# One core, a two-block network: the experts' gate and up products with 512 columns, and partial sums joined by products with stacked identities

## The chip, the cores and the metric

The kernel runs on one core of one Trainium2 chip. The metric is the device time of one launch in microseconds (us). Engines: TensorE (PE in the profile, PEld its weight loads), VectorE (DVE), ScalarE (ACT), GpSimd (POOL), SyncE (SP, which here issues nearly all transfers from memory).

## What is computed

256 tokens of width 1024 pass through two blocks. The first ends in a mixture of 32 experts, which is what the change touches; the second (retention and pooling, feed-forward, convolution, feed-forward) follows it. Each token goes to 2 of the 32 experts:

```python
xb = xf[toks]
hid = jax.nn.silu(xb @ w_exp_gate[e]) * (xb @ w_exp_up[e])
return hid @ w_exp_down[e]
```

Here `xb` is (tokens, 1024), gate and up are (1024, 512), down is (512, 1024), all in 32-bit floats. The three weights of one expert are 6 MB, those of all experts 201 MB, and every launch reads all of them.

## The kernel before

Every expert gets 32 slots (CAP); a branch after the eighth expert (LAST = 7, lines 1667 to 1670) handles experts with more tokens and is not entered with these inputs. For four experts together `gather` (line 1533) builds a one-hot matrix `oh` and turns 4 x 32 token rows into the stationary operand `xe` with the model width on the partitions: eight slices of 128 rows, 32 columns for each expert. `scales` (line 1555) makes the row scale and the gate weight of every slot.

**Gate and up.** `inward` (line 1571) runs once for gate (columns 0:128 of the bank `gu`) and once for up (128:256), and takes two loads of 1 MB each time (`kh`, half of the 1024 rows). TensorE's array is used as four quarters of 32 columns. Before the change quarter n of the array makes output columns n of four: each of the 8 row slices is loaded as weights into all four quarters and each quarter multiplies 128 weight columns. That is 32 products of 128 columns for gate and 32 for up, for each expert; a product in 32-bit floats is two instructions in the trace. The result has the 32 slots of quarter n on partitions 32n to 32n+31. Silu on ACT (line 1657) and a product on DVE (line 1658) make `hd`; `turn` (line 1580) transposes it with one product and a DVE copy to `ht`, the stationary operand of the down product.

**Down.** `down` (line 1587) takes two loads, 16 products of 256 columns in all. `scaled` (line 1594) splits the result into a rounded part (ACT, line 1599) and the rest (DVE, line 1600), four times each, in turn. Once for four experts `scatter` (line 1608, tile `wt`) and `add` (line 1616) put the rows back to their tokens in the banks `y`.

**Order.** The loop over experts runs gate(e), turn(e-1), up(e), then `finish(e-1)`, that is down(e-1). A scheduler sets the order of instructions on each engine inside the loop by its own estimates; an engine then takes them strictly in that order. From line 1675 on (`manual_schedule`) the order is as written: the tail of expert 31 and the start of the retention stage. Between the loop and the tail `tables` (line 1686) computes the sine tables on DVE and ACT (18 DVE instructions, lines 1692 to 1706).

**Loads.** `expert_loads` (line 1508) gives the order of the 1 MB loads: gate, gate, up, up of expert e, then down, down of expert e-1; the very last load is cut in two. SP issues them (line 295) into a ring of 1 MB places, as soon as the place's former content has been used. PSUM has four banks (`pw`) for all of this besides the four `y` banks, taken in turn; the pool `hid` holds one buffer each of `hd`, `ht` and `wt`.

Of the kernel before, what the change touches and what calls it, by code (L numbers as in the profile page):

```python
# [11 lines left out]
AF = mybir.ActivationFunctionType  # L12
OP = mybir.AluOpType
# [7 lines left out]
LAST = 7  # L21
# [142 lines left out]
class Block:  # L164
# [1362 lines left out]
    def experts(self):  # L1527
# [43 lines left out]
        def inward(xe, pg, at):  # L1571
            for kh in range(2):
                w = self.next_weights().rearrange("p k (h c t) -> p k h t c", h=2, t=2)
                for k in range(4):
                    for n in range(4):
                        nc.tensor.matmul(pg[quarter(n), at:at + 128], lhsT=xe[:, 4 * kh + k],  # L1576
                                         rhs=w[:, k, n // 2, n % 2], start=(at == kh == k == 0),
                                         stop=(at > 0 and kh == 1 and k == 3))

        def turn(hd):  # L1580
            pt = self.bank("hT")
            nc.tensor.transpose(pt[:, 0:128], hd, c("ident"))
            ht = tile(self.hid, "ht", 256)[:, 0:128]
            nc.vector.tensor_copy(ht, pt[:, 0:128])
            return ht

        def down(ht, pd, half, ahead=0):
            wd = self.next_weights(ahead)
            for k in range(2):
                for n in range(4):  # L1590
                    nc.tensor.matmul(pd[n % 2][quarter(n), 0:256], lhsT=ht[:, quarter(2 * half + k)],  # L1591
                                     rhs=wd[:, k, n * 256:(n + 1) * 256], start=(half + k == 0), stop=(half == k == 1))

# [8 lines left out]
        def outward(e, ht, gs, ye):  # L1602
            pd = [self.bank("dn")] * 2
            for half in range(2):
                down(ht, pd, half, len(self.places) - 2 if e == LAST and half else 0)
# [18 lines left out]
        group = None  # L1624

        def finish(e, ht, oh, gs):
# [5 lines left out]
            outward(e, ht, gs, group)  # L1632
# [3 lines left out]
        hd = mine = None  # L1636
        for e in range(32):
            of = mine
# [8 lines left out]
            xs = xe[:, :, quarter(e % 4)]  # L1647
            pg = self.bank("gu")
            inward(xs, pg, 0)
            if e % 4 == 0:  # L1650
                gs, scale = scales(e, oh)
                mine = oh, gs
            ht = None if hd is None else turn(hd)
            inward(xs, pg, 128)
            now = tile(self.hid, "hd", 256)[:, 0:128]
            sc = scale[:, e % 4:e % 4 + 1]
            nc.scalar.activation(now, pg[:, 0:128], AF.Silu, scale=sc)  # L1657
            nc.vector.scalar_tensor_tensor(now, pg[:, 128:256], sc, now, op0=OP.mult, op1=OP.mult)  # L1658
            if e == 31:
                nc.gpsimd.tensor_tensor(self.rows[:, 1], self.rows[:, 0], self.rows[:, 1], op=OP.mult)  # L1660
            if ht is not None:
                finish(e - 1, ht, *of)
            hd = now
# [691 lines left out]
```

## Time and profile before

| | |
|---|---|
| median of 3 runs | 1380.73 us (1380.12 to 1380.96) |
| profiled execution | 1378.72 us |
| its span | 1376.8 us, so 1.9 us lie outside it |
| PE busy | 1230.7 us (89%) |
| PE weight loads | 1023.2 us (74%) |
| DVE busy | 769.3 us (56%) |
| ACT busy | 539.6 us (39%) |
| expert weights read | 201 MB of 355 MB |
| PE products of gate and up (line 1576) | 4096 instructions, 168.9 us busy |

The page divides the span into 40 slices of 34 us. A row of windows gives, for each stretch, the busy time of each engine with the number of instructions in brackets, then the granted clock of TensorE as a share of 2.4 GHz, the busy share of the DMA engines and the rate of transfers. A row of a timeline gives start and length in us, engine, line, operation, tiles, how often, and in square brackets how long the engine had been idle before and what it waited for. The expert stage lies between about 347 and 791 us.

### The profile page before, as it was taken

The numbers are of one execution on the slowest core, as the hardware profiler recorded it, in microseconds if no ns is written. First come the engines' busy times: TensorE is split into PE (matmuls) and PEld (weight loads), VectorE is DVE, ScalarE is ACT, GpSimd is POOL, SyncE is SP. The second block draws the span as 40 slices with busy tenths as digits, with TensorE's granted clock in tenths as the row PEclk, the third lists the DMA queues.
The fourth block names the chain that finished last, engine by engine and source line by source line (L and its number), as shares of the span: only waits on it lengthen the run. The fifth ranks groups of instructions, "written<-read, shape, count | busy, mean of one in ns | idle before, by whom it ended". The sixth has DMA issues, their size and how long they took to land.

```text
span 1376.8 us, 28610 instructions
## 1 busy us (share of the span) xinstructions
PE 1230.7 (89%) x12204; PEld 1023.2 (74%) x12204; DVE 769.3 (56%) x1559; ACT 539.6 (39%) x884; POOL 147.0 (11%) x124
## 2 busy tenths in 40 slices
PE   8999999999886777676767699999999999999997
PEld 7989888898765455444535499788888997888886
DVE  5577547876332132131212386877776789766665
ACT  4553533554221111121111274354555535555553
POOL 1022201002000000000000032012221200111112
PEclk9999989999997877888868799999999999999999
DMA  7535513996999999999999998365556268665520
GB/s 213 184 115 158 159 40 128 356 411 253 385 417 416 418 418 420 418 419 418 419 419 418 381 301 292 102 230 184 184 192 190 78 162 266 207 195 195 191 77 31
DMA packets 146455, 360.10 MB, mean 262 GB/s; under 512 B 6672, under 2 KB 101904, under 8 KB 121744
## 3 DMA queue, kind: packets, MB, share of 16 engines
q1 hardware_dynamic: 144800, 353.69, 69.5%
q0 software_dynamic: 1376, 4.25, 1.0%
q8 instruction: 97, 1.59, 0.5%
q14 instruction: 38, 0.31, 0.1%
q10 hardware_dynamic: 144, 0.26, 0.0%
HBM read 354.92 MB, written 3.26 MB: 260 GB/s over the span
## 4 chain that ended last, share of the span: by engine, by line
PE 41%; DMA 24%; DVE 3%; ACT 1%; issue 0%; SPq 0%; ACTq 0%; DVEq 0%
PE f L445 11%; DMA raw<-in_w_exp_down_dram 10%; DMA raw<-in_w_exp_gate_dram 7%; DMA raw<-in_w_exp_up_dram 6%; PE f L446 6%; PE f L468 3%; PE f L467 3%; PE f L469 3%; PE cv L2105 2%; PE first L452 1%; PE v L469 1%; PE v L467 1%; PE v L468 1%; PE gu L1576 1%; PE xe L1545 1%; PE r L468 1%
## 5 line engine op out<-in xcount | busy, mean ns | idle before, releaser
L323 DVE TENSOR_TENSOR wlo<-raw,whi 128x1024 fp32r<-128x1024 f32 x231 | 292.4, 1273 | 151.8 <-ACT whi L321 146.5
L321 ACT ACTIVATE whi<-raw 128x1024 fp32r<-128x1024 f32 x238 | 249.9, 1057 | 220.5 <-PE f L445 87.7
L445 PE MATMUL f<-hT,whi 128*128 128x512 f32 x672 | 236.3, 395 | 0.0
L1576 PE MATMUL gu<-raw,xe 128*32 128x128 f32 x4096 | 168.9, 312 | 53.5 <-DMA raw<-in_w_exp_up_dram 33.4
L1576 PEld LDWEIGHTS gu<-raw,xe 128*32 128x32 f32 x4096 | 130.9, 122 | 92.2 <-DMA raw<-in_w_exp_up_dram 43.4
L446 PE MATMUL f<-hT,wlo 128*128 128x256 f32 x672 | 188.4, 280 | 0.0
L445 PEld LDWEIGHTS f<-hT,whi 128*128 128x128 f32 x672 | 126.0, 188 | 29.4
L1600 DVE SCALAR_TENSOR_TENSOR ye<-dn,gs,ye 32x256 fp32r<-32x256 f32 x128 | 61.5, 481 | 134.5 <-ACT ye L1599 133.8
L1599 ACT ACTIVATE ye<-dn,gs 32x256 fp32r<-32x256 f32 x128 | 59.6, 465 | 174.8 <-PE dn L1591 118.3
L446 PEld LDWEIGHTS f<-hT,wlo 128*128 128x128 f32 x672 | 127.0, 189 | 0.8
L1591 PE MATMUL dn<-raw,ht 128*32 128x256 f32 x1024 | 85.1, 460 | 45.3 <-DMA raw<-in_w_exp_down_dram 37.7
L1591 PEld LDWEIGHTS dn<-raw,ht 128*32 128x32 f32 x1024 | 34.2, 124 | 82.2 <-DMA raw<-in_w_exp_down_dram 29.6
L1658 DVE SCALAR_TENSOR_TENSOR hd<-gu,scale,hd 128x128 f32<-128x128 f32 x32 | 11.2, 350 | 106.6 <-ACT hd L1657 106.5
L1657 ACT ACTIVATE hd<-gu,scale 128x128 f32<-128x128 f32 x32 | 11.8, 367 | 149.8 <-PE gu L1576 149.8
L1948 POOL TENSOR_TENSOR fs<-fs,r 128x512 f32<-128x512 f32 x22 | 39.3, 1787 | 290.0 <-ACT fs L1947 290.0
L467 PE MATMUL f<-whi,fa 128*128 128x512 f32 x176 | 69.3, 394 | 0.0
L468 PE MATMUL f<-whi,fa 128*128 128x512 f32 x176 | 69.0, 392 | 0.2 <-DVE fa L342 0.2
L469 PE MATMUL f<-wlo,fa 128*128 128x512 f32 x176 | 68.7, 390 | 0.0
L1545 PEld LDWEIGHTS xe<-oh,xn 128*128 128x128 f32 x256 | 36.8, 231 | 12.9 <-issue 12.1
L1545 PE MATMUL xe<-oh,xn 128*128 128x128 f32 x256 | 39.0, 320 | 6.5 <-PEq L1669 5.7
L429 PE MATMUL gt<-hT,whi 128*128 128x256 f32 x128 | 38.7, 303 | 0.0
L467 PEld LDWEIGHTS f<-whi,fa 128*128 128x128 f32 x176 | 33.1, 188 | 7.6 <-ACT fa L341 0.5
(618 smaller groups left out, 2547.3 us busy)
## 6 DMA issues: line engine op xcount, KB each, us to landing
raw<-in_w_exp_gate_dram SPq DMA_DIRECT2D x64, 1024.0 KB, 19.9
raw<-in_w_exp_up_dram SPq DMA_DIRECT2D x64, 1024.0 KB, 19.9
raw<-in_w_exp_down_dram SPq DMA_DIRECT2D x63, 1024.0 KB, 20.0
raw<-in_ffn_w_gate_dram SPq DMA_DIRECT2D x22, 1024.0 KB, 5.4
raw<-in_ffn_w_up_dram SPq DMA_DIRECT2D x22, 1024.0 KB, 5.3
raw<-in_ffn_w_down_dram SPq DMA_DIRECT2D x22, 1024.0 KB, 4.8
raw<-in_w_in_dram SPq DMA_DIRECT2D x20, 1024.0 KB, 5.3
raw<-in_conv_w_pw_dram SPq DMA_DIRECT2D x12, 1024.0 KB, 5.5
```

The lines of the kernel that those rows point to most:

```text
L321: nc.scalar.activation(hi, raw[:, k:k + step], AF.Copy)
L323: self.los.append(eng.tensor_tensor(lo, raw[:, k:k + step], hi.bitcast(F32), op=OP.subtract))
L445: nc.tensor.matmul(ps[cb], lhsT=whi[:, k, s], rhs=self.two[n][:, :, kk], start=f, stop=False)
L446: nc.tensor.matmul(ps[cb][:, 1], lhsT=wlo[:, k, s], rhs=self.two[n][:, 0, kk], start=False, stop=l)
L467: nc.tensor.matmul(ps[tt], lhsT=hi[:, k0 + k, s], rhs=whi[:, k, cols], start=f, stop=False)
L468: nc.tensor.matmul(ps[tt], lhsT=lo[:, k0 + k, s], rhs=whi[:, k, cols], start=False, stop=False)
L469: nc.tensor.matmul(ps[tt], lhsT=hi[:, k0 + k, s], rhs=wlo[:, k, cols], start=False, stop=l)
L1545: nc.tensor.matmul(ps[:, a], lhsT=xn[:, tt, d * 128:(d + 1) * 128], rhs=oh[:, tt].rearrange("p e s -> p (e s)"), start=(tt == 0), stop=(tt ...
L1576: nc.tensor.matmul(pg[quarter(n), at:at + 128], lhsT=xe[:, 4 * kh + k], rhs=w[:, k, n // 2, n % 2], start=(at == kh == k == 0), stop=(at > ...
L1591: nc.tensor.matmul(pd[n % 2][quarter(n), 0:256], lhsT=ht[:, quarter(2 * half + k)], rhs=wd[:, k, n * 256:(n + 1) * 256], start=(half + k = ...
L1599: nc.scalar.activation(hi, part, AF.Copy, scale=gs[q])
L1600: nc.vector.scalar_tensor_tensor(lo, part, gs[q], hi.bitcast(F32), op0=OP.mult, op1=OP.subtract)
```

## The change

Gate and up are computed with the other split. Quarter k of the array now takes row slice k of the four in a load, and multiplies all 512 weight columns; so a load needs 4 products of 512 columns instead of 16 of 128. Each quarter then holds a partial sum over a quarter of the rows, in a bank of its own for gate (`pg`) and for up (`pu`). `joined` copies half a bank (256 columns, every second one, with the row scale) to `hd` in SBUF, on ACT for gate and on DVE for up, and returns two products: 128 columns of the copy as the stationary operand, times the constant `rep4`, four identities of 32 stacked on the partitions. Such a product adds the four quarters and turns the result at once. `hidden` applies silu on ACT and the product with up on DVE, and gives `ht` directly; `turn` is gone. `both` runs all of that for one expert, with the down product of the expert before it between the two halves of up (`outward` and `finish` have become generators for this). The loads, their order and their number are the same.

```diff
@@ -1568,20 +1568,30 @@
                 nc.vector.tensor_copy(gs[quarter(a)], ps[quarter(a), a:a + 1])
             return gs, scale
 
-        def inward(xe, pg, at):
-            for kh in range(2):
-                w = self.next_weights().rearrange("p k (h c t) -> p k h t c", h=2, t=2)
+        def inward(xe, pg, halves=(0, 1)):
+
+            for kh in halves:
+                w = self.next_weights()
                 for k in range(4):
-                    for n in range(4):
-                        nc.tensor.matmul(pg[quarter(n), at:at + 128], lhsT=xe[:, 4 * kh + k],
-                                         rhs=w[:, k, n // 2, n % 2], start=(at == kh == k == 0),
-                                         stop=(at > 0 and kh == 1 and k == 3))
-
-        def turn(hd):
-            pt = self.bank("hT")
-            nc.tensor.transpose(pt[:, 0:128], hd, c("ident"))
+                    nc.tensor.matmul(pg[quarter(k)], lhsT=xe[:, 4 * kh + k], rhs=w[:, k], start=(kh == 0), stop=(kh == 1))
+
+        def joined(e, ps, pg, h, by_act):
+
+
+            p = tile(self.hid, "hd", 256)
+            src, sc = pg[:, h * 256:h * 256 + 256].rearrange("p (c t) -> p t c", t=2), scale[:, e % 4:e % 4 + 1]
+            view = p.rearrange("p (t c) -> p t c", t=2)
+            if by_act:
+                nc.scalar.activation(view, src, AF.Copy, scale=sc)
+            else:
+                nc.vector.tensor_scalar(view, src, sc, None, op0=OP.mult)
+            return lambda: [nc.tensor.matmul(ps[:, quarter(2 * h + t)], lhsT=p[:, t * 128:(t + 1) * 128], rhs=c("rep4"),
+                                             start=True, stop=True) for t in range(2)]
+
+        def hidden(ps):
             ht = tile(self.hid, "ht", 256)[:, 0:128]
-            nc.vector.tensor_copy(ht, pt[:, 0:128])
+            nc.scalar.activation(ht, ps[:, 0:128], AF.Silu)
+            nc.vector.tensor_tensor(ht, ht, ps[:, 128:256], op=OP.mult)
             return ht
 
         def down(ht, pd, half, ahead=0):
@@ -1590,6 +1600,20 @@
                 for n in range(4):
                     nc.tensor.matmul(pd[n % 2][quarter(n), 0:256], lhsT=ht[:, quarter(2 * half + k)],
                                      rhs=wd[:, k, n * 256:(n + 1) * 256], start=(half + k == 0), stop=(half == k == 1))
+
+        def both(e, xs, between=lambda: None, then=lambda: None):
+            pg, pu, ps = self.bank("gu"), self.bank("gu"), self.bank("hT")
+            inward(xs, pg)
+            between()
+            for h in range(2):
+                add = joined(e, ps[:, 0:128], pg, h, True)
+                inward(xs, pu, (h,))
+                add()
+            for h in range(2):
+                add = joined(e, ps[:, 128:256], pu, h, False)
+                then()
+                add()
+            return hidden(ps)
 
         def scaled(e, pd, gs, ye):
             q = quarter(e % 4)
@@ -1601,8 +1625,9 @@
 
         def outward(e, ht, gs, ye):
             pd = [self.bank("dn")] * 2
-            for half in range(2):
-                down(ht, pd, half, len(self.places) - 2 if e == LAST and half else 0)
+            down(ht, pd, 0)
+            yield
+            down(ht, pd, 1, len(self.places) - 2 if e == LAST else 0)
             scaled(e, pd, gs, ye)
 
         def scatter(oh):
@@ -1629,13 +1654,13 @@
                 group = tile(self.ye, "ye", 2048, F32R).rearrange("p (m d) -> p m d", m=2)
             if e % 4 == 3:
                 wt = scatter(oh)
-            outward(e, ht, gs, group)
+            yield from outward(e, ht, gs, group)
             if e % 4 == 3:
                 add(e - 3, wt, group)
 
-        hd = mine = None
+        ht = mine = None
         for e in range(32):
-            of = mine
+            of, steps = mine, iter(())
             if e % 4 == 0:
                 xe, oh = gather(e)
                 if not e:
@@ -1644,27 +1669,25 @@
                 self.rows = self.beside("rows", self.t8).rearrange("p (n d) -> p n d", n=2)
                 for n, ap in enumerate((i["norm_final"], i["mixer_norm_g_2"][0])):
                     nc.gpsimd.dma_start(out=self.rows[:, n], in_=ap.partition_broadcast(128))
-            xs = xe[:, :, quarter(e % 4)]
-            pg = self.bank("gu")
-            inward(xs, pg, 0)
-            if e % 4 == 0:
-                gs, scale = scales(e, oh)
-                mine = oh, gs
-            ht = None if hd is None else turn(hd)
-            inward(xs, pg, 128)
-            now = tile(self.hid, "hd", 256)[:, 0:128]
-            sc = scale[:, e % 4:e % 4 + 1]
-            nc.scalar.activation(now, pg[:, 0:128], AF.Silu, scale=sc)
-            nc.vector.scalar_tensor_tensor(now, pg[:, 128:256], sc, now, op0=OP.mult, op1=OP.mult)
+
+            def between():
+                nonlocal gs, scale, mine
+                if e % 4 == 0:
+                    gs, scale = scales(e, oh)
+                    mine = oh, gs
+
+            gs, scale = (None, None) if e == 0 else (gs, scale)
+            if ht is not None:
+                steps = finish(e - 1, ht, *of)
+            ht = both(e, xe[:, :, quarter(e % 4)], between, lambda: next(steps, None))
+            for _ in steps:
+                pass
             if e == 31:
                 nc.gpsimd.tensor_tensor(self.rows[:, 1], self.rows[:, 0], self.rows[:, 1], op=OP.mult)
-            if ht is not None:
-                finish(e - 1, ht, *of)
-            hd = now
             if e == LAST:
-                finish(e, turn(hd), *mine)
-                hd = None
-            if e == LAST:
+                for _ in finish(e, ht, *mine):
+                    pass
+                ht = None
                 most = nc.values_load(self.most[0:1, 0:1], min_val=0, max_val=T)
                 with self.tc.If(most > CAP):
                     self.overflow()
@@ -1675,7 +1698,7 @@
         self.region = self.tc.manual_schedule(engines={PE, ACT, DVE, POOL})
         self.region.__enter__()
         oh, gs = mine
-        ht, wt = turn(hd), scatter(oh)
+        wt = scatter(oh)
         pd = [self.bank("dn") for _ in range(2)]
         for half in range(2):
             down(ht, pd, half)
```

On PE this is expert 30, with no gather in it (two gate loads, two up loads, the two down loads of expert 29; `gu`, `hT`, `dn` are the PSUM banks, `raw` a load), before:

```order
L1576 MATMUL gu<-raw,xe 32x128 x16
L1582 MATMUL hT<-cst,hd 128x128
L1576 MATMUL gu<-raw,xe 32x128 x48
L1591 MATMUL dn<-raw,ht 32x256 x16
```

and with the change:

```order
L1576 MATMUL gu<-raw,xe 32x512 x12
L1588 MATMUL hT<-cst,hd 128x32 x4
L1576 MATMUL gu<-raw,xe 32x512 x4
L1588 MATMUL hT<-cst,hd 128x32 x4
L1601 MATMUL dn<-raw,ht 32x256 x16
```

The gate and up products have gone from 64 to 16; one transpose has become eight products with `rep4`, in two places with four in a row, and all of them stand ahead of the down products of the expert before.

On PE the end of the stage, from the gate and up products of expert 31 on, before:

```order
L1576 MATMUL gu<-raw,xe 32x128 x16
L1582 MATMUL hT<-cst,hd 128x128
L1576 MATMUL gu<-raw,xe 32x128 x48
L1591 MATMUL dn<-raw,ht 32x256 x8
L1582 MATMUL hT<-cst,hd 128x128
L1611 MATMUL wt<-cst,oh 128x128 x2
L1591 MATMUL dn<-raw,ht 32x256 x24
L1620 MATMUL y_3917<-ye,wt 128x512
```

and with the change:

```order
L1576 MATMUL gu<-raw,xe 32x512 x12
L1588 MATMUL hT<-cst,hd 128x32 x4
L1576 MATMUL gu<-raw,xe 32x512 x4
L1588 MATMUL hT<-cst,hd 128x32 x4
L1601 MATMUL dn<-raw,ht 32x256 x8
L1636 MATMUL wt<-cst,oh 128x128 x2
L1601 MATMUL dn<-raw,ht 32x256 x24
L1645 MATMUL y_3917<-ye,wt 128x512
```

The transpose of expert 31 that stood between the two halves of down(30) is gone, and eight products with `rep4` stand ahead of both halves, four of them behind all of up.

On DVE the same end of the stage, from the last instructions of the sine tables (`raw`) on, before:

```order
L1700 SCALAR_TENSOR_TENSOR raw<-raw 128x256
L1701 SCALAR_TENSOR_TENSOR raw<-raw 128x256
L1704 TENSOR_SCALAR raw<-raw 128x256
L1706 TENSOR_SCALAR raw<-raw,cst 128x256
L1658 SCALAR_TENSOR_TENSOR hd<-gu,scale,hd 128x128
L1584 COPY ht<-hT 128x128
L1600 SCALAR_TENSOR_TENSOR ye<-dn,gs,ye 32x256 x8
L1718 TENSOR_TENSOR xg<-y_3917,rows 128x512
```

and with the change:

```order
L1723 SCALAR_TENSOR_TENSOR raw<-raw 128x256
L1724 SCALAR_TENSOR_TENSOR raw<-raw 128x256
L1727 TENSOR_SCALAR raw<-raw 128x256
L1729 TENSOR_SCALAR raw<-raw,cst 128x256
L1587 TENSOR_SCALAR hd<-gu,scale 128x256 x2
L1624 SCALAR_TENSOR_TENSOR ye<-dn,gs,ye 32x256
L1594 TENSOR_TENSOR ht<-ht,hT 128x128
L1624 SCALAR_TENSOR_TENSOR ye<-dn,gs,ye 32x256 x7
L1741 TENSOR_TENSOR xg<-y_3917,rows 128x512
```

Behind the tables stood the product that makes `hd` of expert 31; now the two copies of up's halves stand there, and the product that makes `ht` comes behind the first `ye` instruction of expert 30.

## Rows read from the trace of the kernel before

**Rows 1.** The page, part 2: 40 slices of the span, busy tenths.

```profile
DMA  7535513996999999999999998365556268665520
```

**Rows 2.** Windows: busy of PE, PEld, DVE, ACT, POOL; granted clock; DMA share; GB/s.

```profile
700.00:750.00 50.00, 36.71 (x581) 25.50 (x585) 11.41 (x39) 7.66 (x17) 0.00 (x0) 0.80 1.01 418
...
780.00:785.00 5.00, 4.35 (x51) 2.28 (x43) 3.15 (x10) 1.20 (x3) 0.00 (x0) 0.50 0.90 344
785.00:790.00 5.00, 3.68 (x45) 1.41 (x48) 1.73 (x4) 1.90 (x5) 0.00 (x0) 0.86 0.87 304
```

**Rows 3.** Chain of waits that ended last: start, length, what; 454 to 791 us.

```profile
454.73 19.84 DMA raw<-in_w_exp_down_dram
...
772.22 17.54 DMA raw<-in_w_exp_down_dram
789.80 0.71 PE dn L1591 x8
```

**Rows 4.** Waits of SP, 340 to 360 us: us in total, times, longest.

```profile
SPq L295 <- PE gu L1576: 16.1, 6, 12.0
```

**Rows 5.** Windows of 1 us at the first expert, columns as in rows 2.

```profile
351.00:352.00 1.00, 1.00 (x34) 0.96 (x37) 0.35 (x2) 0.41 (x1) 0.00 (x0) 1.00 0.12 49
352.00:353.00 1.00, 1.00 (x40) 0.84 (x32) 0.00 (x0) 0.00 (x0) 0.00 (x0) 1.00 0.02 8
```

**Rows 6.** Timeline of PE at the first two experts, 350 to 364 us.

```profile
350.61 0.31 PE L1454 MATMUL count<-row,cst 128*128 128x32 f32 x2
350.75 0.39 PE L1455 MATMUL count<-row,cst 128*128 128x32 f32 x2
351.07 2.05 PE L1576 MATMUL gu<-raw,xe 128*32 128x128 f32 x64
353.05 0.61 PE L1559 MATMUL gs<-chosen,oh 128*128 128x4 f32 x4
...
357.88 0.33 PE L1582 MATMUL hT<-cst,hd 128*128 128x128 f32 x1
358.14 2.05 PE L1576 MATMUL gu<-raw,xe 128*32 128x128 f32 x64
360.01 1.91 PE L1591 MATMUL dn<-raw,ht 128*32 128x256 f32 x32
361.73 2.44 PE L1576 MATMUL gu<-raw,xe 128*32 128x128 f32 x64
```

**Rows 7.** Timeline of all engines at the stage's end, experts 30 and 31.

```profile
774.75 1.77 PE L1576 MATMUL gu<-raw,xe 128*32 128x128 f32 x32 [0.16 <-DMA raw<-in_w_exp_gate_dram]
...
776.59 0.29 DVE L1692 CAST raw<-pos 128x256 f32<-128x256 int32 x1 [0.95 <-PE gu L1576]
...
779.74 1.93 PE L1576 MATMUL gu<-raw,xe 128*32 128x128 f32 x32 [1.38 <-DMA raw<-in_w_exp_up_dram]
...
783.17 0.36 DVE L1706 TENSOR_SCALAR raw<-raw,cst 128x256 f32<-128x256 f32 x1 [0.48 <-ACT raw L1705]
...
783.56 0.35 DVE L1658 SCALAR_TENSOR_TENSOR hd<-gu,scale,hd 128x128 f32<-128x128 f32 x1
...
784.19 0.48 PE L1582 MATMUL hT<-cst,hd 128*128 128x128 f32 x1
...
784.46 0.63 PE L1611 MATMUL wt<-cst,oh 128*128 128x128 f32 x2
...
785.02 1.75 PE L1591 MATMUL dn<-raw,ht 128*32 128x256 f32 x16
...
789.80 0.64 PE L1591 MATMUL dn<-raw,ht 128*32 128x256 f32 x8 [0.68 <-DMA raw<-in_w_exp_down_dram]
...
790.37 2.65 DVE L1600 SCALAR_TENSOR_TENSOR ye<-dn,gs,ye 32x256 fp32r<-32x256 f32 x5 [0.53 <-ACT ye L1599]
```

**Rows 8.** Groups by line, 400 to 860 us: busy, mean ns of one, idle before.

```profile
L1584 DVE COPY ht<-hT 128x128 f32<-128x128 f32 x27 | 7.9, 292 | 23.7 <-PE hT L1582 19.7 <-PE dn L1591 3.6
...
L1550 DVE COPY xe<-xe 128x512 f32<-128x512 f32 x6 | 4.1, 692 | 32.7 <-PE xe L1545 32.7
```

## The prediction, made before the changed kernel ran

> **What bounds the kernel now.** I read the page's slices first, then windows, then the chain of waits, then SP's waits and the timeline at both ends of the expert stage. The slices show the DMA engines full in fourteen slices in a row, where the experts are [rows 1]. Windows inside say it in numbers: from 700 to 750 us the DMA share is 1.01 at 418 GB/s, while PE is busy 36.7 of 50 us at a granted clock of 0.80 (it goes between full, 2.4 GHz, and half, 1.2), DVE 11.4 and ACT 7.7 [rows 2]. The chain agrees: from 454.73 us on it runs through expert loads, and leaves them only at 789.80 us, for the last eight instructions of the last down product [rows 3]. So the stage lasts as long as its bytes: six loads of 1 MB (1.05 million bytes each) for one expert, 6.29 MB at 418 GB/s, 15.05 us; 2.5 us for one load. What PE does in between counts only in two places: at the start, where the transfers wait for the first free places, and at the end, behind the last loads.
>
> At the start SP waits 16.1 us for the gate and up products of line 1576, once 12.0 us [rows 4]: the ring is full until the first expert has used its first load. The DMA engines then stand nearly still, at shares of 0.12 and 0.02 in the microseconds from 351 to 353 [rows 5]. That gap of 2 us is all the stream has to gain.
>
> **The products.** Prices at full clock come from the first two experts [rows 6]. Now 64 instructions of 128 columns take 1.98 us (351.07 to 353.05), 31 ns each, so a load (32) 0.99 and an expert (128) 3.96. The down products, 256 columns on the same four quarters, take 1.72 us for 32 (360.01 to 361.73), 53.8 ns each. With 512 columns I take twice that, 107.5 ns: eight instructions for a load, 0.86 us, 3.44 for an expert. That is 0.52 less. The transpose took 0.26 (357.88 to 358.14) and goes. The four joins come: each is two products with 128x128 weights and 32 columns, four instructions. The nearest row has that very form, the four instructions of the two `count` lines with the way back to the quarters, 0.46 us (350.61 to 351.07). Four joins are 1.84. So PE has 0.52 + 0.26 = 0.78 less and 1.84 more, 1.06 us more for each expert, at full clock.
>
> At one place a rule speaks against the change. The row shows 0.26 us for a single transpose between two runs of quarter products, while one of the `count` instructions takes 0.46 / 4 = 0.115, so at most 0.15 us goes into changing from quarters to the whole array and back; the change does this four times in an expert instead of once [rows 6]. The Trainium skill (TensorEngine Tiling (Array Packing), Tiling Modes) says that a change of the tiling mode drains the engine. The trace agrees with a small price; by it two joins at the end would be up to 0.3 us dearer, which the range below holds anyway.
>
> **In the stage.** These 1.06 us lie beside the loads: a plain expert took PE 3.96 + 0.26 + 1.72 = 5.9 us and takes 7.0, of 15.05. At half clock it is 14.0, and the joins add waits, since `hd` has one buffer and PE must wait there for ACT or DVE to copy. A copy of 128x256 from PSUM lies between 0.29 us (128x128) and 0.69 (128x512), by columns 0.43 [rows 8]. Four of these with handovers are some 2.4 us, so at half clock PE would need about 16.4 and fall behind a little; it then stands idle less, and in these rows the clock comes back after full stretches (0.50, then 0.86) [rows 2]. I cost the stage at nothing: the cover is the 15.05 us of loads. Without it the price would be 32 x 1.06 = 34 us. ACT's and DVE's added copies are free in the same way.
>
> **At the start** the first place comes free after eight instructions instead of 32, 0.86 us for 0.99: the stream starts 0.13 us earlier, and everything behind it. Bounds are 0 and -0.13, since no place can be free before the first product has run. I take -0.1. Places two to four come free within 0.5 us of where they did, and 2.5 us of transfer for each covers that.
>
> **At the end** there is no cover. Before, DVE works through the sine tables from 776.59 us, when the second gate load of expert 31 is used up (774.75 + 1.77 = 776.52), to 783.53 [rows 7]. The up products were done at 781.67, yet `hd` starts at 783.56: it stands behind the tables on DVE. What follows is short, because the first half of down(30) does not need it; the second half ends at 785.02 + 1.75 = 786.77, and from there the `ye` instructions, ACT and DVE in turn, set the end: the last one of DVE ends at 793.02, 6.25 us later [rows 7]. The last load arrives at 789.80 and only just does not matter.
>
> With the change the two copies of up stand at the place of `hd` behind the tables, each with its join, and **both halves of down(30) stand behind the second join on PE**. So I count from the end of the tables to the end of down(30). The tables start when the second gate load is used up: at half clock 0.86 x 2 = 1.72 us after 774.75, as now, end 783.5; at full clock 0.86 after, end 782.6. I take 783.0. Then come two copies, 0.86; two joins, 0.92 at full clock, 1.84 at half if everything doubles, between them 1.4 (the transposes `wt` cost 0.56 for two at half clock, 784.46 to 785.02, hardly more than the single one at full); the first half of down(30), 0.86 or 1.75; `wt`, 0.28 or 0.56; the second half, 0.86 or 1.75; and four handovers. One is 0.28 us (DVE's `hd` ends at 783.91, PE starts at 784.19), one 0.03 (783.53 to 783.56); I take 0.15 each, 0.6.
>
> - All at full clock: 782.6 + 0.86 + 0.92 + 0.86 + 0.28 + 0.86 + 0.6 = 787.0, 0.2 us later than 786.77.
> - All at half clock: 783.5 + 0.86 + 1.84 + 1.75 + 0.56 + 1.75 + 0.6 = 790.9, 4.1 later.
> - Half clock up to the first half of down(30), full behind it: 783.0 + 0.86 + 1.4 + 1.75 + 0.28 + 0.86 + 0.6 = 788.75, 2.0 later.
>
> I take the third: the clock is 0.50 from 780 to 785 now and 0.86 in the next 5 us [rows 2], and PE has more waits there than before. Silu and the product for `ht` fit into the gaps between the `ye` instructions of ACT and DVE, and down(31) is ready before its `ye` turn comes, so the 6.25 us stay. Behind them nothing is changed, and the next stage starts from these rows, so the delay goes through. Sum: -0.1 + 2.0 = +1.9 us. Made against the profiled 1378.72 us (span 1376.8) it gives 1380.6; the median of the runs stands 2.0 above that execution, and I add the difference to the median: 1380.73 + 1.9 = **1382.6**.
>
> **Rivals.**
> - *The added products keep the clock up.* Then the end costs 0.2 us and the start gives back 0.1: 1380.8, no change. For it: the clock rises after busy stretches in these rows, and PE has 1.06 us more to do for an expert. Against it: from 776 to 783 PE would wait for loads and copies. The Trainium skill (TensorE: Matmul & The Clock Gate, Why this matters for your kernels) advises to keep TensorE continuously busy and free of gaps; by it the added products would hold the clock up to the end, and the time would be this rival's; no run here shows that yet.
> - *Slower, by the tail at half clock.* Both joins and both down halves at half clock, 4.1 us; if down(31) runs at half clock too, its 1.72 us for a half come twice behind `ht`, and the `ye` of expert 31 wait another 1.3. That gives 1384.7 to 1386.0. It decides from a delay of 2.8 us on, which is 0.2%, about what a measurement of this kernel can tell from no change. For it: 0.50 now at just that place.
> - *The four quarters do not run side by side with 512 columns.* Then one instruction takes 0.43 us (107.5 x 4) and an expert 32 x 0.43 = 13.8 instead of 3.4: PE needs 17.4 us or more against 15.05, and the stage grows by 32 x 2.3 = 75 us. Against it: the down products do run side by side at 256 columns.
> - *Faster.* The tail gets shorter only if down(30) no longer stands behind the tables, and the start gap of 2 us only closes with an earlier first product. Neither is in the change.
>
> **How the numbers follow.** Forecast 0.52 (1380.9 to 1384.1), clock stays up 0.20, tail at half clock 0.22, quarters in a row 0.02, faster for a reason I do not see 0.04. Of the forecast's share about 0.09 lies above +2.8 us. Slower: 0.22 + 0.02 + 0.09 = 0.33; faster 0.04; same 0.63. The range leaves out the quarters in a row and the far ends of both sides: 1379.5 to 1386.0.
>
> **What would show it.** In the changed kernel's trace: eight instructions of 512 columns in about 0.86 us at full clock; a DMA share near 1.0 from 354 us to the last load and that load within 0.3 us of 789.8; the first copy of up for expert 31 right behind the sine tables on DVE; the end of down(30) at 788 to 790; and the whole delay of the last `ye` found again at the span's end. It is wrong if the last load itself moves by over 1 us, if SP waits for products in the middle of the stage, or if down(30) ends before 786.8.

## The result, and the profile after

The changed kernel took 1396.43 us, the median of four runs (1387.28 to 1400.24), beside 1380.42 us for the kernel before: a ratio of 1.0113 [1.0089, 1.0137], 16 us slower. The forecast was 1382.6 with a range up to 1386.0, so the time lies outside, on the slow side, and no rival gave it either. The profiled execution, the slowest of the four, took 1400.24 us; its span is 1398.4 us, 21.6 more than the 1376.8 of before.

The page of the changed kernel, part 2 (40 slices of the span; the clock granted to TensorE and the DMA share) and part 4 (shares of the chain that ended last):

```profile
PEclk9999989999996997676788799999999999999999
DMA  6545515987999999999999767365556358655620
...
PE 39%; DVE 4%; ACT 2%; DMA 1%; issue 1%; DVEq 0%; ACTq 0%; SPq 0%
```

The DMA engines are full through the experts' slices, as in [rows 1], but transfers no longer carry the chain: 1% of the span, where [rows 3] run from load to load for 335 us. Windows of the changed kernel, columns as in [rows 2]:

```profile
700.00:750.00 50.00, 41.74 (x312) 22.09 (x312) 13.03 (x34) 12.03 (x28) 3.47 (x3) 0.83 1.01 418
...
785.00:790.00 5.00, 5.00 (x40) 2.71 (x44) 0.00 (x0) 0.30 (x1) 0.00 (x0) 0.50 1.03 323
...
795.00:800.00 5.00, 1.63 (x12) 0.68 (x12) 4.43 (x14) 0.54 (x2) 0.00 (x0) 0.82 0.05 17
800.00:805.00 5.00, 3.18 (x20) 2.46 (x24) 1.32 (x3) 0.29 (x1) 0.00 (x0) 0.50 0.00 0
```

From 700 to 750 us the stream is as full as before (1.01, 418 GB/s). By 795 to 800 us it is empty (0.05). In the trace the last expert load is issued at 767.70 us and lands 17.6 us later, at 785.3, 4.5 us *earlier* than before (789.75); PE then still has all the products of expert 31 and the down products of experts 29 and 30 ahead of it. So the loads were in time and PE was late. PE's waits between 351 and 790 us show when that came about (us in all, times, longest). Before:

```profile
PE dn L1591 <- DMA raw<-in_w_exp_down_dram: 37.7, 34, 2.8
PE gu L1576 <- DMA raw<-in_w_exp_up_dram: 33.4, 30, 2.7
PE gu L1576 <- DMA raw<-in_w_exp_gate_dram: 17.3, 22, 1.4
```

and the changed kernel:

```profile
PE hT L1588 <- DVE hd L1587: 25.3, 41, 0.7
PE hT L1588 <- ACT hd L1585: 22.0, 30, 1.6
```

PE waited 88.4 us for loads before, and now not once for long enough to be listed; it waits 47.3 us for the copies into `hd`. **PE's spare time, 88.4 us or 2.8 for an expert, was used up.** Groups by line over 16 experts show by what (from expert 12 to expert 28; busy us, mean ns, idle before). Before, 486.5 to 729.9 us:

```profile
L1576 PE MATMUL gu<-raw,xe 128*32 128x128 f32 x2020 | 90.4, 329 | 36.1 <-DMA raw<-in_w_exp_up_dram 23.5 <-DMA raw<-in_w_exp_gate_dram 12.3
L1591 PE MATMUL dn<-raw,ht 128*32 128x256 f32 x512 | 44.7, 476 | 26.3 <-DMA raw<-in_w_exp_down_dram 25.0 <-DVE ht L1584 1.2
L1545 PE MATMUL xe<-oh,xn 128*128 128x128 f32 x128 | 20.3, 323 | 0.0
L1620 PE MATMUL y<-ye,wt 128*128 128x512 f32 x32 | 11.8, 472 | 4.8 <-ACT ye L1599 4.8
L1582 PE MATMUL hT<-cst,hd 128*128 128x128 f32 x16 | 5.6, 349 | 0.0
```

and the changed kernel, 499 to 747.6 us:

```profile
L1576 PE MATMUL gu<-raw,xe 128*32 128x512 f32 x508 | 73.1, 678 | 0.0
L1601 PE MATMUL dn<-raw,ht 128*32 128x256 f32 x512 | 50.8, 555 | 0.0
L1588 PE MATMUL hT<-cst,hd 128*128 128x32 f32 x256 | 48.9, 320 | 34.2 <-DVE hd L1587 17.9 <-ACT hd L1585 15.8 <-DVE ye L1624 0.5
```

The products fell from 90.4 to 73.1 us, the transposes' 5.6 went, the joins cost 48.9 busy and 34.2 of waiting, and the unchanged down products rose from 44.7 to 50.8 at a lower clock (0.77 for 0.80). In all PE was busy 173.0 us of 243.4 before and 205.3 of 248.6 after: 2.0 us more for an expert, and 2.1 more of waits ahead of joins. The two together, 4.1, are more than these same experts waited for loads before: 60.8 us (23.5 + 12.3 + 25.0), 3.8 for an expert, beside the stage's mean of 2.8. The 0.3 beyond is what the pace shows: 248.6 / 16 = 15.5 us for an expert, before 243.4 / 16 = 15.2.

These 16 experts are not the whole loss. Compare the start of the first gate-weight product (`gs`) of an expert in the two traces: that of expert 8 comes 20.8 us later than before (462.94 for 442.11), that of expert 12 12.6, of expert 16 8.0, of expert 28 17.7. PE falls behind already ahead of the branch, makes up a part behind it, and loses it again.

### The profile page after: what moved, and what is told of

It reads as the page before. It is cut to its first block, busy times and chain, and to the rows that moved or that the text cites. A ratio compares the mean times of both kernels' runs of the same rounds, so it can differ in the third digit from the quotient of the medians.

```text
span 1398.4 us, 23663 instructions
## 1 busy us (share of the span) xinstructions
PE 1292.4 (92%) x9612; PEld 1001.4 (72%) x9612; DVE 787.8 (56%) x1591; ACT 566.5 (41%) x948; POOL 147.2 (11%) x124
## 5 line engine op out<-in xcount | busy, mean ns | idle before, releaser
L1588 PEld LDWEIGHTS hT<-cst,hd 128*128 128x128 f32 x512 | 78.5, 219 | 129.3 <-DVE hd L1587 66.9
L1576 PE MATMUL gu<-raw,xe 128*32 128x512 f32 x1024 | 144.3, 655 | 0.0
L1588 PE MATMUL hT<-cst,hd 128*128 128x32 f32 x512 | 92.5, 308 | 54.4 <-DVE hd L1587 30.5
L1601 PE MATMUL dn<-raw,ht 128*32 128x256 f32 x1024 | 94.7, 517 | 2.9 <-issue 2.9
L1587 DVE TENSOR_SCALAR hd<-gu,scale 128x256 f32<-128x256 f32 x64 | 30.9, 484 | 116.3 <-PE gu L1576 65.9
L1576 PEld LDWEIGHTS gu<-raw,xe 128*32 128x32 f32 x1024 | 29.3, 118 | 48.4 <-issue 36.5
L1585 ACT ACTIVATE hd<-gu,scale 128x256 f32<-128x256 f32 x64 | 30.4, 474 | 68.3 <-PE gu L1576 28.1
L1545 PEld LDWEIGHTS xe<-oh,xn 128*128 128x128 f32 x256 | 38.5, 240 | 11.8 <-issue 10.9
```

The source lines that it names most:

```text
L1545: nc.tensor.matmul(ps[:, a], lhsT=xn[:, tt, d * 128:(d + 1) * 128], rhs=oh[:, tt].rearrange("p e s -> p (e s)"), start=(tt == 0), stop=(tt ...
L1576: nc.tensor.matmul(pg[quarter(k)], lhsT=xe[:, 4 * kh + k], rhs=w[:, k], start=(kh == 0), stop=(kh == 1))
L1588: return lambda: [nc.tensor.matmul(ps[:, quarter(2 * h + t)], lhsT=p[:, t * 128:(t + 1) * 128], rhs=c("rep4"), start=True, stop=True) for ...
```

## Where one expert loses the time

The changed kernel on PE and on the engines that make `hd`, one plain expert in the scheduler's order (timeline, columns as in [rows 7]):

```profile
643.61 0.47 ACT L1585 ACTIVATE hd<-gu,scale 128x256 f32<-128x256 f32 x1 [0.91 <-PE hT L1588]
644.14 0.63 PE L1588 MATMUL hT<-cst,hd 128*128 128x32 f32 x4 [0.62 <-ACT hd L1585]
644.70 1.06 PE L1576 MATMUL gu<-raw,xe 128*32 128x512 f32 x8
645.89 0.48 DVE L1587 TENSOR_SCALAR hd<-gu,scale 128x256 f32<-128x256 f32 x1 [8.38 <-PE gu L1576]
646.43 0.63 PE L1588 MATMUL hT<-cst,hd 128*128 128x32 f32 x4 [0.67 <-DVE hd L1587]
647.10 0.48 DVE L1587 TENSOR_SCALAR hd<-gu,scale 128x256 f32<-128x256 f32 x1 [0.72 <-PE hT L1588]
647.64 0.71 PE L1588 MATMUL hT<-cst,hd 128*128 128x32 f32 x4 [0.58 <-DVE hd L1587]
648.28 3.48 PE L1601 MATMUL dn<-raw,ht 128*32 128x256 f32 x32
```

The two joins of up stand one behind the other. The first needs a copy that cannot start before up's last product, the second one that cannot start before the first join has read the single `hd`; so PE stands still 0.67 and 0.58 us, with both halves of the down product, ready to run, queued behind. The granted clock changes in the next stretches. Windows of 1 us behind it, the changed kernel:

```profile
649.00:650.00 1.00, 1.00 (x14) 0.40 (x10) 0.00 (x0) 0.00 (x0) 0.00 (x0) 0.50 1.03 426
650.00:651.00 1.00, 1.00 (x16) 0.54 (x12) 0.00 (x0) 0.00 (x0) 0.00 (x0) 0.50 1.00 418
...
652.00:653.00 1.00, 1.00 (x16) 0.36 (x12) 0.66 (x2) 0.62 (x3) 0.00 (x0) 1.00 1.02 426
...
655.00:656.00 1.00, 0.11 (x1) 0.11 (x2) 0.48 (x1) 0.81 (x2) 0.00 (x0) 1.00 1.02 426
...
659.00:660.00 1.00, 0.35 (x5) 0.23 (x2) 0.48 (x1) 0.00 (x0) 0.00 (x0) 0.50 1.05 434
```

The gaps fall into microseconds at full clock, and the dense down product behind them (649 to 651) gets half. The clock comes back behind it (652) just as the next wait comes (655), and is gone at 659. So it was 0.77 over these 16 experts, 0.80 before, although PE was busy 83% of the time and not 71% (206.7 and 178.4 us of the 250 from 500 to 750).

## The experiments

Four theories. WAITS: the waits for `hd`, set by the order, use up PE's time. PRICE: the joins themselves do. CLOCK: half clock doubles what PE has to do, and without it there would be room. TAIL: the sine tables ahead of the last joins. Each run stands beside runs of the kernel before in its own session. "Pace" is the time from the first gate-weight product (`gs`) of expert 0 to that of expert 28, divided by 28, in the profiled execution.

| run | median us | ratio to before | span | pace | clock 500 to 750 |
|---|---|---|---|---|---|
| before | 1380.42 | | 1376.8 | 13.46 | 0.81 |
| the change | 1396.43 | 1.0113 [1.0089, 1.0137] | 1398.4 | 14.13 | 0.77 |
| written order | 1374.19 | 0.9979 [0.9962, 0.9996] | 1373.4 | 13.52 | 0.80 |
| written order, again | 1377.41 | 0.9994 [0.9984, 1.0004] | 1375.7 | 13.46 | 0.79 |
| joins back to back | 1405.72 | 1.0178 [1.0155, 1.0201] | 1405.9 | 14.34 | 0.83 |
| no branch | 1415.25 | 1.0275 [1.0233, 1.0318] | 1411.3 | 14.66 | 0.76 |
| two buffers, no branch | 1380.72 | 1.0004 [0.9991, 1.0016] | 1377.2 | 13.30 | 0.81 |
| half joins | 1379.00 | 0.9989 [0.9979, 0.9998] | 1375.7 | 13.45 | 0.81 |
| three dummies a join | 1387.21 | 1.0045 [1.0022, 1.0068] | 1386.4 | 13.66 | 1.00 |
| written order, four dummies | 1386.12 | 1.0042 [1.0027, 1.0058] | 1384.6 | 13.89 | 0.99 |
| no tables | 1395.42 | 1.0113 [1.0059, 1.0167] | 1397.1 | 14.14 | 0.77 |
| written order, no tables | 1376.77 | 0.9991 [0.9980, 1.0003] | 1373.7 | 13.46 | 0.84 |

**PE's order as written.** Nothing else is changed; one half of down(e-1) then stands ahead of each join of up.

```diff
-            ht = both(e, xe[:, :, quarter(e % 4)], between, lambda: next(steps, None))
-            for _ in steps:
-                pass
+            with self.tc.manual_schedule(engines={PE}):
+                ht = both(e, xe[:, :, quarter(e % 4)], between, lambda: next(steps, None))
+                for _ in steps:
+                    pass
```

> The changed kernel with PE's order in the expert loop as it is written (gate, half of up, join, half of up, join, half of down, join, half of down, join) instead of the scheduler's order, which puts two joins back to back from expert 13 on. Theory WAITS: PE became the bound of the stage because in back-to-back joins it waits 0.6 us each time for the copy into the one buffer hd, and at half clock besides; it needs 16.2 us for an expert there against 15.05 us of loads. In the written order the copies lie beside other products, a plain expert takes 8 us (as experts 9 to 11 do in the changed kernel), PE catches up and waits for loads again: 1381 to 1387 us. Rival PRICE: the joins' own instructions are too dear in any order: no change, 1390 to 1400 us.

The loss is gone with the same instructions and the same prices; 1374.19 us is even below the expected interval. One expert of this kernel, PE's timeline at half clock:

```profile
635.23 1.06 PE L1588 MATMUL hT<-cst,hd 128*128 128x32 f32 x4
636.22 1.94 PE L1576 MATMUL gu<-raw,xe 128*32 128x512 f32 x8
638.09 1.06 PE L1588 MATMUL hT<-cst,hd 128*128 128x32 f32 x4
639.08 1.94 PE L1601 MATMUL dn<-raw,ht 128*32 128x256 f32 x16
640.95 1.06 PE L1588 MATMUL hT<-cst,hd 128*128 128x32 f32 x4
641.94 1.94 PE L1601 MATMUL dn<-raw,ht 128*32 128x256 f32 x16
643.81 1.06 PE L1588 MATMUL hT<-cst,hd 128*128 128x32 f32 x4
```

Each copy lies beside a run of products and no row has an idle time in brackets. From 351 to 790 us PE waits 5.6 us for ACT's copies, none for DVE's that is listed, and 38.1 for loads again. The clock (0.80) is no better than before, so here it was not the clock that was mended. (In the changed kernel, joins stand back to back ahead of the branch, too, at 406.08 and 407.28 us for example, not only from expert 13 on.)

> The written order once more, beside the run without tables and with more rounds: 1372 to 1376 us, ratio to before 0.996 to 0.999. If the gain over the kernel before was scatter between sessions: 1378 to 1381.

1377.41 us lies between the two expectations: the loss stays away, but the small gain over the kernel before is not there a second time. I read the two runs as no change against it.

**The scheduler's order of up's joins, by hand.** PE's order is written out as above, with one line less, so that both down halves stand behind both joins of up. The two joins of gate keep half of up between them, and no expert is set densely, so it is not the scheduler's order throughout:

```diff
             for h in range(2):
                 add = joined(e, ps[:, 128:256], pu, h, False)
-                then()
                 add()
```

> The run with PE's order written out (joins of up with half a down product between them) gave 1374.2 us. Here PE's order is written out too, with the same instructions, but both halves of the down product stand behind both joins of up, as the scheduler of the changed kernel sets them. If the loss comes from the order (PE waits for the copy into the one buffer `hd` with nothing to do in between, falls behind the loads, and its clock falls): 6 to 22 us more than the written order, 1380 to 1396, copies waited for by PE some 15 to 40 us in all, and experts 16 to 28 at 15.3 to 16.3 us each. If the loss comes from something else that the hand-written region took away with it (the handling of instructions at region ends, other engines' order, transfers issued at another time): within 3 us of the written order, 1371 to 1377.

It lost 31.5 us against the written order (28.3 against its second run; 25 to 28 by the ratios to the kernel before), more than expected, by moving one piece of work. PE's waits from 351 to 790 us:

```profile
PE hT L1588 <- DVE hd L1587: 33.8, 56, 0.6
PE hT L1588 <- ACT hd L1585: 19.6, 19, 1.9
```
 The hand-written region is not what helped; the place of the down product is. The clock from 500 to 750 us is 0.83, above that of the kernel before (0.81), so a low clock in that stretch is not what lost the time here. The surprise is the pace: from expert 12 to 28 it is 14.6 us, *below* the 15.05 of an expert's loads, and not 15.3 or more. PE lost time against a shorter budget than I had (below).

**No branch.** The branch behind expert 8, not entered here, is left out.

```diff
-                most = nc.values_load(self.most[0:1, 0:1], min_val=0, max_val=T)
-                with self.tc.If(most > CAP):
-                    self.overflow()
```

> The changed kernel without the branch for experts with more than 32 tokens (not entered with these inputs; its test and its code are left out). PE stands still 5.3 us at the branch and has drained its queue ahead of it. If the backlog at the end is one that PE carries along from there (BRANCH), 8 to 16 us less, 1381 to 1389. WAITS: PE loses 1.1 us for every expert from the sixteenth on whatever went before, but starts from a smaller backlog: 3 to 8 us less. PRICE says the same as WAITS.

Meant to save the 5.3 us that PE waits at the branch, it cost 19 us; no theory had that. In the changed kernel the scheduler starts afresh behind the branch and sets experts 8 to 12 densely (36.1 us for the four, 462.94 to 499.03); without it their joins stand back to back, and the four take 55.0 (446.72 to 501.74). So the order WAITS speaks of spread, and this run speaks for it by accident.

**Two buffers for `hd`, no branch.** In the kernel of the last run (`ht` is made narrower, and the pool of small tiles has ten places for twelve):

```diff
-            p = tile(self.hid, "hd", 256)
+            p = self.hid.tile([128, 256], F32, name="hd", tag="hd", bufs=2)
```

> As the run without the branch after expert 8 (1415.3 us), which is not entered with these inputs, and with two buffers for `hd` in place of one; to make room for it `ht` is 128 columns wide and the pool of small tiles has 10 places in place of 12. If the waits for the copy into the single buffer are the cause: PE's waits for `hd` fall from about 2.5 to below 1 us for an expert, experts 16 to 28 come to 15.05 to 15.4 us each, 1378 to 1395 us. If the price of the joins themselves is the cause (PE short of time at any order): 1410 to 1418, experts still at 16 us or more.

From 1415.25 to 1380.72 us: 34.5 us, in the scheduler's own order. Two copies now run one after the other ahead of two joins in a row; PE's waits for them fall from 57.1 us (351 to 790) to 27.6, and 25.6 us of waits for loads are back. WAITS holds in both orders. The narrower `ht` and the smaller pool came with the second buffer and were not tried alone.

**Half the joins.** One product of 64 columns in place of two of 32; half of the hidden columns is left wrong.

```diff
-            return lambda: [nc.tensor.matmul(ps[:, quarter(2 * h + t)], lhsT=p[:, t * 128:(t + 1) * 128], rhs=c("rep4"),
-                                             start=True, stop=True) for t in range(2)]
+            at = CST["rep4"][0]
+            return lambda: nc.tensor.matmul(ps[:, 64 * h:64 * h + 64], lhsT=p[:, 0:128], rhs=self.cst[:, at:at + 64],
+                                            start=True, stop=True)
```

> The changed kernel, where a join is one product of 64 columns in place of two of 32; the second 128 columns of the copy are not used, so part of the hidden values is left wrong and two instructions out of four of each join are left out. It takes 4 times about 0.28 us (full clock) to 0.53 us (half) from every expert. If PE is short of time in the second half of the stage, each expert there ends 1.1 to 2.1 us sooner until the loads bound it again (15.05 us for 16.2): 1379 to 1388 us. If the waits alone matter and the products of a join are hidden within them: within 3 us of the changed kernel, 1393 to 1400.

1379.0 us, at the lower end of PRICE's interval, with the waits left almost as they were (41.7 us for `hd`). So PRICE holds as well: taking either away is enough. It is a threshold, not one cause.

**Dummy products.** Three products of 128x128 identities ahead of each join, results unused, in the scheduler's order:

```diff
+                for _ in range(3):
+                    nc.tensor.matmul(idle[:, 256:384], lhsT=c("ident"), rhs=c("ident"), start=True, stop=True)
                 for t in range(2):
                     nc.tensor.matmul(ps[:, quarter(2 * h + t)], lhsT=p[:, t * 128:(t + 1) * 128], rhs=c("rep4"),
                                      start=True, stop=True)
```

> The changed kernel with three more products (128x128 with itself, into an unused part of the bank hT) ahead of every join, 0.35 us at full clock, 0.7 at half, nothing else changed. If the half clock that comes with the waits is what makes PE slow (part of WAITS), products in the gaps of 0.6 us keep the clock up and the kernel gets faster by 4 us or more, 1383 to 1392. If it is the waits alone or the price of the joins (PRICE), 4 x 0.35 us for each expert come on top where they don't fit into a gap: 1396 to 1430 us.

About 3 us more work for each expert, and the kernel is 9 us faster than the change. The window of 500 to 750 us:

```profile
500.00:750.00 250.00, 231.66 (x2106) 146.86 (x2098) 77.39 (x240) 60.25 (x137) 3.48 (x3) 1.00 1.01 419
```

PE is busy 231.66 us of 250 at full clock, where the change has 206.65 at 0.77. So CLOCK has its part: what the waits cost is paid twice, once as idle time and once as half clock behind it. It is a part only: at full clock the kernel is still 8 us above the one before in its session (1378.97), and no run has the full clock without added products. The Trainium skill (TensorE: Matmul & The Clock Gate, Why this matters for your kernels) advises to keep TensorE busy continuously; this run agrees, with 1.00 for 0.77 and 9 us. The next one sets its limit.

**Four dummies in the written order.**

> PE's order written out, and four products of 128x128 identities added before each join, results unused. In the scheduler's order three such products made the kernel 9 us faster by the clock (1.00 from 500 to 750 us). Here the loads already bound the stage (PE waits 38 us for them). If the clock only matters where PE is late: 1372 to 1377, the same as the written order, with a clock nearer to 1.00; at most 1 to 2 us less by a faster tail (down(31) there ran at half clock, 3.3 us). If the added products take more than the clock gives back: 1377 to 1385.

The clock is 0.99 and the time 12 us above the written order (9 above its second run), just beyond the upper case: the products cost more than the clock gave. Eight such instructions take 1.0 us, four times for an expert, and a plain expert takes 11.5 us at full clock (427.70 to 439.23 in its trace). With the work of every fourth expert that is a pace of 13.89, just above the 13.46 of the kernel before, which waits for loads; PE here is listed with no wait for a load, so the dummies themselves made it late. In these two runs a higher clock was worth something only where PE was late without the dummies.

**The tables.** Two copies stand in place of the sine tables' arithmetic, so the rotation later gets wrong values.

> The changed kernel without the arithmetic of the sine tables (16 of 18 DVE instructions and both sines left out, so the tables' values are missing). The forecast's own mechanism, TAIL: the tables lie on the path at the end, 6.9 us (793.76 to 800.68 in the changed kernel's trace), so 6 to 7 us less, 1387 to 1391. If the end is set by PE's backlog alone and the tables fit beside it, under 2 us less.

1395.42 for 1396.43 us. With PE some 20 us behind, the end of the tables is one more wait among many: from the start of down(29) to the end of down(30) the profiled execution takes 17.9 us for 22.3, but it reached the start of down(29) 1.9 us later, and the runs of either kernel scatter by 13 us. By these two profiles the tables account for some 4 of the 21.6 us; TAIL is not the main cause, and an effect of that size lies below this scatter.

> PE's order written out, where PE keeps up with the loads, and the arithmetic of the sine tables left out: two copies stand in its place, so the rotation that uses the tables later gets wrong values, and 16 DVE and 2 ACT instructions at the end of the expert stage are left out. In the scheduler's order the same omission changed nothing, since PE was some 20 us behind there. If the tables set the tail once the loads bound the stage (the two copies of up stand behind them, with their joins, and half of down(30) behind that): 1.5 to 3 us less than the written order, 1371 to 1373. If the last loads set the tail at that point: within 0.7 us of the written order.

Where PE keeps up, the same omission is worth 0.6 us (1376.77 for 1377.41, with intervals that overlap): the second expectation. Without the tables down(30) waits for its loads (0.97 and 0.51 us), so the last loads stand right behind the tables in that place.

## Why the prediction was wrong, step by step

**The step that failed** is "I cost the stage at nothing: the cover is the 15.05 us of loads". It had the right parts and compared them wrongly, in three ways.

*The budget.* 15.05 us is the time of an expert's loads, but not what PE has for an expert. In the traces of both kernels SP issues 22 loads of the experts before 351 us, and the stream then stands still for want of a place [rows 4, 5]: the ring is full when the stage starts. These 22 are 55 us of transfer that PE gets for nothing, 2.0 for each of the first 28 experts. Before, PE went through 28 experts in 13.46 us each, waits for loads included. The runs fit this roughly: 32 times the pace beyond 13.46 gives 21 us for the change (span +21.6), 28 for the joins back to back (+29.1), 38 without the branch (+34.5), 6 for three dummies (+9.6), 14 for four (+7.8). It is no law: the four dummies are 6 us off, and two buffers, at 13.30, gained nothing (+0.4). And the pace holds the delay itself; it shows that the time is lost among the experts, not by what. The ring also hides the loss: it absorbs PE's delay, the stream runs on at 1.01, the last load is even 4.5 us early, and the delay is seen only behind it.

*The need.* "A plain expert took PE 5.9 us and takes 7.0" leaves out every fourth expert's work: gather 20.3 us, `y` 11.8, `gs` 5.0 and `wt` 2.1 in 16 experts before, 2.45 us for each. The waits I had at "some 2.4 us", and measured 2.1 (34.2 / 16); I named them and charged nothing for them. What I should have put beside each other stood in the trace: PE's 2.8 us of waits for loads an expert, against 1.06 (full clock) to 2.1 (half) of work and 2.4 of waits. My own sizes say 3.5 to 4.5 against 2.8. Even by my own sum the need at half clock, 16.4 us, was above the 15.05; I set that aside with the clock.

*The clock.* "It then stands idle less and the clock comes back" was wrong: 0.77 for 0.80. PE was idle less in all, but in the gaps at the joins, and the rows above show half clock behind each. In these rows dense products bring it back; a PE that was merely busier did not.

**Prices.** The first rows of the changed kernel's PE timeline that answer to [rows 6]:

```profile
350.18 1.92 PE L1576 MATMUL gu<-raw,xe 128*32 128x512 f32 x16
352.03 0.61 PE L1559 MATMUL gs<-chosen,oh 128*128 128x4 f32 x4
...
354.38 0.63 PE L1588 MATMUL hT<-cst,hd 128*128 128x32 f32 x4 [0.30 <-ACT hd L1585]
354.94 1.07 PE L1576 MATMUL gu<-raw,xe 128*32 128x512 f32 x8
```

Sixteen instructions take 1.85 us to the next row, 0.925 for a load: 0.86 was 7% low, and the saving is half of what I had. A join takes 0.56 and not 0.46, so the row of the same form was 0.1 us short, within the 0.15 that I had left for the change from quarters to the whole array and back. A copy of 128x256 takes 0.47 to 0.48 us where I had 0.43 from [rows 8]. With 0.925 and 0.56 a plain expert costs 1.7 us more at full clock, not 1.06. The rival of quarters in a row is refuted by the same rows.

**The start.** Windows of the changed kernel, as in [rows 5]:

```profile
350.00:351.00 1.00, 1.00 (x11) 0.42 (x14) 0.35 (x2) 0.51 (x1) 0.00 (x0) 1.00 0.28 115
351.00:352.00 1.00, 1.00 (x12) 0.13 (x4) 0.00 (x0) 0.00 (x0) 0.00 (x0) 1.00 0.04 16
352.00:353.00 1.00, 1.00 (x12) 0.97 (x8) 0.00 (x0) 0.00 (x0) 0.00 (x0) 1.00 0.94 139
```

The gap is still there; whether it is the 0.1 us shorter that I said is too small to read from these rows.

**The tail.** The mechanism is there, but it did not make the loss. Timeline of the changed kernel, which answers to [rows 7]:

```profile
800.32 0.35 DVE L1729 TENSOR_SCALAR raw<-raw,cst 128x256 f32<-128x256 f32 x1 [0.48 <-ACT raw L1728]
800.71 0.48 DVE L1587 TENSOR_SCALAR hd<-gu,scale 128x256 f32<-128x256 f32 x1
801.25 1.06 PE L1588 MATMUL hT<-cst,hd 128*128 128x32 f32 x4 [4.60 <-DVE hd L1587]
...
806.37 1.94 PE L1601 MATMUL dn<-raw,ht 128*32 128x256 f32 x16
...
812.90 2.34 PE L1645 MATMUL y<-ye,wt 128*128 128x512 f32 x8 [1.20 <-ACT ye L1623]
```

The copy stands right behind the tables, as foreseen, but at 800.7, since PE released the tables' place that late. Its size is better read where the loads bind. The kernel with two buffers and no branch, PE's timeline:

```profile
770.70 1.06 PE L1531 MATMUL gu<-raw,xe 128*32 128x512 f32 x8 [1.34 <-DMA raw<-in_w_exp_gate_dram]
...
779.54 1.91 PE L1543 MATMUL hT<-cst,hd 128*128 128x32 f32 x8 [0.61 <-DVE hd L1542]
...
783.87 1.94 PE L1556 MATMUL dn<-raw,ht 128*32 128x256 f32 x16
...
791.54 2.32 PE L1600 MATMUL y<-ye,wt 128*128 128x512 f32 x8 [1.05 <-ACT ye L1578]
```

From the last gate product to the end of down(30) (785.8) it takes 15.1 us, before 12.0 [rows 7]: 3.1 longer, within my bounds of 0.2 to 4.1. Yet `y` starts at 791.54, as it did before (791.49 in its chain of waits), because that gate load was used 4 us earlier (770.70 for 774.75). From 350 to 770 us this kernel moved 175.1 MB and the one before 174.5, which at 418 GB/s is 1.5 us, and its last load lands at 785.72 us, 4.0 earlier. In the one profile of each of the eleven runs with the change the last load lands 1.7 to 7.3 us earlier than in the one of the kernel before; why stays open.

**The signs I gave.** "A DMA share near 1.0" held and proved nothing, since the ring hides a late PE. That "the last load itself moves by over 1 us" came true, but by 4.5 us to the *early* side, so in these profiles the stream gained more than the gap of 2 us that I allowed it. Down(30) ends at 808.3 us and not at 788 to 790. "SP waits for products in the middle" was the right alarm: between 400 and 770 us SP waits 11.1 us for gate and up products after, 1.9 before (between 340 and 800, the start included, 34.7 and 18.6, and 116.8 with the joins back to back).

## What to carry to other kernels

When work is added to an engine under a stream, compare the added work *and the added waits* with that engine's own waits for the stream over the whole stage (88.4 us here), not with the time of one load, and count the work of the occasional step, too. Here a ring filled ahead shortened the engine's budget and hid its delay until the stream ended. A join through a single buffer belongs in an order where other work of the same engine stands between two joins: here that alone was worth some 25 to 31 us, and a second buffer about 35.

## What the runs showed of the hardware that I had not expected

Gaps of 0.6 to 1.6 us between products were followed by stretches at half clock, in which dense products ran about twice as long (3.48 us for the 32 of a down product, where [rows 6] have 1.72); a PE 83% busy had a lower clock (0.77) than one 71% busy (0.80). Filling gaps with idle products made a late kernel 9 us faster and one that was in time 9 to 12 us slower. An instruction of 32 columns with 128x128 weights takes 0.14 us at full clock (0.56 / 4), beside 0.116 for one of 512 columns with four quarters side by side (0.925 / 8). A join of few columns was not cheap: four joins, 2.24 us, took more than half of what all the gate and up products of an expert take (3.7).
